# Another number of identity passes behind column sums, LRU gates and SSD products in a two-block sequence model

## The chip, the cores and the metric

The kernel runs on one core of one Trainium2 chip. The metric is the device time of one launch in microseconds, and the time of a kernel is the median of its runs. Engines are called TensorE (PE; its weight loads are PEld), VectorE (DVE), ScalarE (ACT), GpSimd (POOL) and SyncE (SP).

## What is computed

One sequence of 256 tokens with 2048 features goes through two blocks in float32. The first block has two layers: an RG-LRU beside an mLSTM, and an SSD layer. The second block has three branches (S5, gated linear attention, differential attention) and a feed-forward part. In short:

```python
def first_block(x, ...):
    x = x + lru_mlstm_layer(rmsnorm(x, e_norm[0]), ...)
    x = x + ssd_layer(rmsnorm(x, o_norm[0]), ...)
    return rmsnorm(x, final_norm)

def rglru(x, w_a, b_a, w_x, b_x, lam):            # 16 blocks of 128 features
    r = sigmoid(einsum('bsni,nij->bsnj', xb, w_a) + b_a)
    i = sigmoid(einsum('bsni,nij->bsnj', xb, w_x) + b_x)
    log_a = -8 * r * softplus(-lam)
    u = sqrt(-expm1(2 * log_a)) * (i * x)         # then a scan over the sequence

def ssd_scan(xh, dt, a, bm, cm):                  # 8 groups of 8 heads, chunks of 128 tokens
    y_diag = einsum('bcgls,bcgels,bcsgep->bclgep', cb, decay, xdt)
    ...

def rmsnorm(x, w):
    return x * rsqrt(mean(x * x, axis=-1) + 1e-6) * w
```

Nearly all the arithmetic is in the dense projections (`x @ w_in`, `y @ w_out`, the feed-forward matrices): 8048 blocks of 128 by 128 weights.

## The kernel before

Features lie on the partitions, tokens along the free dimension: an activation tile is 128 features by 256 tokens, and `[P, 2, T]` holds two of them. Each block of 128 by 128 weights is one step of `prod` (L285 to L293). Weights come by DMA in chunks of eight blocks (L250), ScalarE rounds four blocks at a time to the short float format (`wh`, L260), VectorE keeps the remainder (`wl`, L261). Activations are split alike, into `xh` and `xl`. A step is three matmuls of 128 x 256 into one PSUM tile `pm`: high by high (L291), high by low (L292), low by high (L293). The word *product* below means one such matmul; there are 3 x 8048 of them, in a fixed order that `_plan` lists.

The smaller work of a layer is written as generators that are put on a list; after each finished output tile `pump` advances each of them by one step, so their matmuls stand between those of the products. Within that, a scheduler sets the final order on each engine: it moves an instruction forward or back by its own estimate of when operands are ready. Its order is fixed when the program is built.

The words for what interrupts the products on TensorE:

- A *column sum* (`colsum`, L370 to L383) adds up squares over the partitions with matmuls of one column against a column of ones (L380). Each such matmul is two instructions in the trace. With `add` VectorE first adds the tiles into one (four instructions in all); without it there are two tiles (eight instructions).
- An *identity pass* (`align`, L389 to L393) transposes the identity into a PSUM tile `ps` that nobody reads. `colsum` ends with some of them, and so does each gate of the RG-LRU (L709).
- A *row pass* (`bcast`, L395 to L401): two transposes (L400) spread the 256 values that came out of a column sum, after a chain of small VectorE work (`rsqrt`), over all partitions.
- A *gate* of the RG-LRU (L697 to L709): matmuls by the two gate matrices (L704, L705).
- The *SSD products* (L1019 to L1028): for each of the eight groups, twice in the loop over `i`, sixteen matmuls that go in pairs to two halves of the array (L1027).

How many identity passes there are is set by three lines: a counter `aligned` runs through the calls, and

```python
        self.align(self.nalign() if add else 4)      # L382, in colsum
        return (1, 2, 4)[self.aligned % 3]           # L387, in nalign
        self.align(self.nalign())                    # L709, in rglru
```

so that successive places get 2, 4, 1, 2, 4, 1 and so on. A column sum without `add` (at the start of a layer, of a block and of the feed-forward part) always gets 4.

Of the kernel before, what the change touches and what calls it, by code (L numbers as in the profile page):

```python
# [150 lines left out]
class Builder:  # L151
    def __init__(self, nc, tc, d, dbg, ctx):
        self.nc, self.tc, self.d, self.dbg = nc, tc, d, dbg
        self.ctx = ctx
        self.uid = 0
        pool = lambda **k: ctx.enter_context(tc.tile_pool(**k))
        self.cst = pool(name="cst", bufs=1)

        self.gap(pool, 320)
        self.wp = pool(name="wp", bufs=1)  # L160
        self.gap(pool, 448)
        self.xp = pool(name="xp", bufs=1)
        self.tp = pool(name="tmp", bufs=1)
        self.gap(pool, 384)
        self.pm = pool(name="pm", bufs=1, space=PSUM)
        self.ps = pool(name="ps", bufs=1, space=PSUM)
        self.dr = pool(name="dr", bufs=1, space=DRAM)
        self.side = []
        self.aligned = 0

        self.plan = []
        at = {}
        for name, n in _plan():
            assert n % CH == 0, name
            for _ in range(n // CH):
                self.plan.append((name, at.get(name, 0)))
                at[name] = at.get(name, 0) + 1
        self.w_dma = 0
        self.w_split = 0
        self.w_pos = 0  # L180
        self.raw, self.hl = {}, {}
# [188 lines left out]
    def colsum(self, tiles, add=True):  # L370

        nc = self.nc
        while add and len(tiles) > 1:
            for i in range(len(tiles) // 2):
                nc.vector.tensor_tensor(tiles[i], tiles[i], tiles[len(tiles) - 1 - i], op=ALU.add)
            tiles = tiles[:len(tiles) // 2]
        p = self.pss((P, 2))
        for h in range(2):
            for i, t in enumerate(tiles):
                nc.tensor.matmul(p[:, h:h + 1], t[:, h * P:(h + 1) * P], self.con("ones", 0, 1),  # L380
                                 start=i == 0, stop=i == len(tiles) - 1)
        self.align(self.nalign() if add else 4)  # L382
        return p  # L383

    def nalign(self):
        self.aligned += 1
        return (1, 2, 4)[self.aligned % 3]  # L387

    def align(self, n):  # L389

# [299 lines left out]
    def rglru(self, i, u, lruw, sp, hb, yl):  # L690

        nc = self.nc
        x = self.tmp()
        for n in range(2):
            j = 2 * i + n
            self.conv(u[:, n], [self.par("conv_l_w", 16 * k + j) for k in range(4)],
                      self.par("conv_l_b", j), 4, x[:, n])  # L697
        yield

        a, g = self.tmp(), self.tmp()  # L700
        for n in range(2):
            j = 2 * i + n
            pr = self.pss()
            nc.tensor.matmul(pr[:, 0], lruw[:, n, 0:P], x[:, n], start=True, stop=True)  # L704
            nc.tensor.matmul(pr[:, 1], lruw[:, n, P:2 * P], x[:, n], start=True, stop=True)  # L705
            nc.scalar.activation(a[:, n], pr[:, 0], AF.Tanh, bias=hb[:, j:j + 1], scale=0.5)
            nc.scalar.activation(g[:, n], pr[:, 1], AF.Tanh, bias=hb[:, 16 + j:17 + j], scale=0.5)
        nc.vector.scalar_tensor_tensor(g, g, 1.0, x, op0=ALU.add, op1=ALU.mult)
        self.align(self.nalign())  # L709
        yield  # L710

        if self.lru is None:
            self.lru = self.st.tile([P, 4, T], F32, name=self.nm("lt"), tag="lt", bufs=1), []
        tt, todo = self.lru
        t = tt[:, 2 * len(todo):2 * len(todo) + 2]
        for n in range(2):
            nc.vector.tensor_scalar(a[:, n], a[:, n], 1.0, sp[:, 2 * i + n:2 * i + n + 1], op0=ALU.add, op1=ALU.mult)
        nc.scalar.activation(t, a, AF.Tanh, scale=-0.5)
        nc.scalar.activation(a, a, AF.Exp)
        nc.vector.scalar_tensor_tensor(g, a, 1.0, g, op0=ALU.add, op1=ALU.mult)  # L720
        todo.append((a, g, t))
        if i in LRU_ROOTS:
            self.lru = None
            yield
            tt = tt[:, 0:2 * len(todo)]
            nc.scalar.activation(tt, tt, AF.Sqrt, scale=0.25)
            for a, g, t in todo:
                nc.vector.tensor_tensor(g, g, t, op=ALU.mult)
                y = self.act()
                for n in range(2):  # L730
                    nc.vector.tensor_tensor_scan(y[:, n], a[:, n], g[:, n], 0.0, op0=ALU.mult, op1=ALU.add)
                yl.append(y)
        yield
# [245 lines left out]
    def ssd(self, g, bc, xs, tk, scr, yd):  # L979
        nc = self.nc  # L980
        csb = self.st.tile([P, 8, T], F32, name=self.nm("csb"), tag="csb", bufs=2)
        nc.gpsimd.dma_start(csb, scr[8 * g:8 * g + 8, :].unsqueeze(0).broadcast_to([P, 8, T]))

        S = self.pss((P, 384))
        nc.tensor.matmul(S[:, 0:256], bc[:, 0, 0:P], bc[:, 1, :], start=True, stop=True)
        nc.tensor.matmul(S[:, 256:384], bc[:, 0, P:T], bc[:, 1, P:T], start=True, stop=True)
        cb = self.act((P, 384))
        nc.vector.tensor_tensor(cb, S, self.con("tri3"), op=ALU.mult)

        xdt = []  # L990
        for hf in range(2):
            p = self.pss((P, 512))
            for i in range(2):
                for n in range(2):
                    c = 2 * i + n
                    nc.tensor.transpose(p[:, c * P:(c + 1) * P], xs[i][:, n, hf * P:(hf + 1) * P], self.con("ident"))  # L996
            o = self.act((P, 512))
            for e in range(8):
                nc.scalar.mul(o[:, 64 * e:64 * e + 64], p[:, 64 * e:64 * e + 64], tk[:, 2 + hf, 8 * g + e:8 * g + e + 1])
            xdt.append(o)  # L1000
        yield
        for i in range(2):
            dcs = []
            for e2 in range(2):
                dc = self.st.tile([P, 2, 384], F32, name=self.nm("dc"), tag="dc", bufs=3)
                for e in range(2):
                    ee = 4 * i + 2 * e2 + e
                    hd = 8 * g + ee

                    nc.vector.tensor_scalar(dc[:, e, 0:P], csb[:, ee, 0:P], tk[:, 0, hd:hd + 1], 0.0,  # L1010
                                            op0=ALU.add, op1=ALU.min)
                    nc.vector.tensor_scalar(dc[:, e, T:], csb[:, ee, P:T], tk[:, 1, hd:hd + 1], 0.0,
                                            op0=ALU.add, op1=ALU.min)
                    nc.scalar.activation(dc[:, e, P:T], csb[:, ee, P:T], AF.Exp, bias=tk[:, 0, hd:hd + 1])
                dv = dc.rearrange("p e (b l) -> p e b l", l=P)[:, :, 0::2, :]
                nc.scalar.activation(dv, dv, AF.Exp)
                nc.vector.tensor_tensor(dc, dc, cb.unsqueeze(1).broadcast_to([P, 2, 384]), op=ALU.mult)
                dcs.append(dc)
            yield  # L1019
            py = self.pss()  # L1020
            for t in range(2):
                for s in range(2):
                    for e in range(2):
                        ee = 4 * i + 2 * t + e
                        o = py[64 * e:64 * e + 64, t, :] if s == 0 else py[64 * e:64 * e + 64, t, P:T]
                        r = dcs[t][:, e, 0:256] if s == 0 else dcs[t][:, e, 256:384]
                        nc.tensor.matmul(o, xdt[s][:, 64 * ee:64 * ee + 64], r, start=s == 0, stop=s == 1,  # L1027
                                         tile_position=(0, 64 * e))  # L1028
            for n in range(2):
                nc.vector.scalar_tensor_tensor(xs[i][:, n], xs[i][:, n], self.par("d_skip", 4 * g + 2 * i + n),  # L1030
                                               py[:, n], op0=ALU.mult, op1=ALU.add)
            yd.append(xs[i])
            yield


# [727 lines left out]
```

## Time and profile before

| | |
|---|---|
| median of 3 runs | 3035.64 us |
| the three runs | 3035.18, 3035.64, 3041.25 us |
| the profiled execution | 3039.45 us, its span 3037.7 us |
| granted TensorE clock over the span | 0.997 |
| busy: TensorE matmul / weight load | 99% / 98% of the span |
| busy: VectorE / ScalarE / GpSimd | 75% / 58% / 3% |
| L260 ScalarE rounding of weights | 2013 times, 622 ns each |
| L261 VectorE remainder | 2013 times, 696 ns each |

How to read it: the first lines are times, the rest comes from one profiled execution. A busy share of 99% doesn't say how fast the engine goes while it is busy: the rows of matmuls overlap, each lasting some 0.28 us while the next begins after less than half of that. How fast it goes is read by counting the instructions in a stretch of known length. The granted clock is a fraction of the full 2.4 GHz.

### The profile page before, as it was taken

Reading aid. Unit: us, or ns where it says so; the run is one execution under the profiler, and the core shown is the slowest. Engines: PE = TensorE matmul, PEld = TensorE weight load, DVE = VectorE, ACT = ScalarE, POOL = GpSimd, SP = SyncE. Lnnn points to the kernel's source line nnn. Section 1 sums busy time; section 2 is a strip of 40 time slices with the busy share of each in tenths; the row PEclk is TensorE's granted clock in tenths of the full one; section 3 lists DMA queues with packets and bytes.
Section 4 is the critical chain, followed back from the end, with each engine's and each line's share of the span. In section 5 each row is a group of like instructions: output and inputs, shape, how many; then the busy total and the mean of one; then the engine's idle time right before and its main releaser. Section 6 shows DMA issues by size and latency. Waiting matters only on the chain.

```text
span 3037.7 us, 67061 instructions
## 1 busy us (share of the span) xinstructions
PE 3012.5 (99%) x26390; PEld 2963.1 (98%) x26390; DVE 2291.7 (75%) x4693; ACT 1748.2 (58%) x3303; POOL 90.4 (3%) x123
## 2 busy tenths in 40 slices
PE   8999999999999999999999999999999999999998
PEld 8999999999999999999999999999999999999998
DVE  8787866779999777778888686676677776577764
ACT  6776545556677555565555554555555555455554
POOL 1000000010000000120000000000010000000000
PEclk9999999999999999999999999999999999999999
DMA  6665556666665556665555554556666666665564
GB/s 232 185 189 164 186 160 194 194 189 213 192 194 181 175 184 191 192 203 180 156 158 160 168 162 153 168 166 215 195 190 188 187 188 187 188 186 186 186 187 152
DMA packets 153933, 556.30 MB, mean 183 GB/s; under 512 B 17392, under 2 KB 18544, under 8 KB 152592
## 3 DMA queue, kind: packets, MB, share of 16 engines
q1 hardware_dynamic: 148752, 534.89, 56.8%
q0 software_dynamic: 3104, 14.75, 1.3%
q8 instruction: 206, 3.38, 0.4%
q10 hardware_dynamic: 1760, 2.38, 0.3%
q14 instruction: 111, 0.91, 0.1%
HBM read 547.69 MB, written 4.26 MB: 182 GB/s over the span
## 4 chain that ended last, share of the span: by engine, by line
PE 98%; DVE 1%; DMA 0%; issue 0%; ACT 0%; SPq 0%; DVEq 0%; ACTq 0%
PE pm L291 31%; PE pm L292 30%; PE pm L293 30%; PE ps L1027 1%; PE ps L1329 0%; PE ps L1367 0%; PE ps L1488 0%; PE ps L380 0%; DVE wl L261 0%; PE ps L393 0%; PE ps L1314 0%; PE ps L1259 0%; PE ps L821 0%; PE ps L996 0%; PE ps L704 0%
## 5 line engine op out<-in xcount | busy, mean ns | idle before, releaser
L260 ACT CAST wh<-w 128x512 fp32r<-128x512 f32 (+1 forms) x2013 | 1237.6, 622 | 1138.8 <-PE pm L292 849.5
L261 DVE TENSOR_TENSOR wl<-w,wh 128x512 fp32r<-128x512 f32 (+1 forms) x2013 | 1387.5, 696 | 587.7 <-ACT wh L260 571.1
L291 PE MATMUL pm<-x,wh 128*128 128x256 f32 x5504 | 1541.9, 280 | 6.0 <-ACT wh L260 5.7
L293 PE MATMUL pm<-x,wl 128*128 128x256 f32 x5504 | 1535.2, 279 | 3.3 <-DVE q L448 3.2
L292 PE MATMUL pm<-x,wh 128*128 128x256 f32 x5504 | 1536.4, 279 | 1.5 <-DVE x L509 1.5
L291 PEld LDWEIGHTS pm<-x,wh 128*128 128x128 f32 x5504 | 1035.4, 188 | 15.1 <-issue 7.9
L293 PEld LDWEIGHTS pm<-x,wl 128*128 128x128 f32 x5504 | 1042.9, 190 | 6.6 <-DVE q L448 3.4
L292 PEld LDWEIGHTS pm<-x,wh 128*128 128x128 f32 x5504 | 1036.1, 188 | 4.1 <-issue 1.9
L291 PE MATMUL pm<-a,wh 128*128 128x256 f32 x1712 | 479.0, 280 | 0.5 <-ACT wh L260 0.5
L292 PE MATMUL pm<-a,wh 128*128 128x256 f32 x1712 | 477.7, 279 | 0.3 <-DVE a L344 0.3
L293 PE MATMUL pm<-a,wl 128*128 128x256 f32 x1712 | 477.9, 279 | 0.0
L293 PEld LDWEIGHTS pm<-a,wl 128*128 128x128 f32 x1712 | 324.6, 190 | 0.1
L291 PEld LDWEIGHTS pm<-a,wh 128*128 128x128 f32 x1712 | 322.0, 188 | 0.9 <-ACT wh L260 0.7
L292 PEld LDWEIGHTS pm<-a,wh 128*128 128x128 f32 x1712 | 321.5, 188 | 0.6 <-DVE a L344 0.5
L291 PE MATMUL pm<-h,wh 128*128 128x256 f32 x576 | 162.4, 282 | 1.8 <-DVE t L1113 1.8
L292 PE MATMUL pm<-h,wh 128*128 128x256 f32 x576 | 161.3, 280 | 0.0
L293 PE MATMUL pm<-h,wl 128*128 128x256 f32 x576 | 161.0, 280 | 0.0
L291 PEld LDWEIGHTS pm<-h,wh 128*128 128x128 f32 x576 | 109.7, 190 | 5.8 <-issue 3.1
L292 PEld LDWEIGHTS pm<-h,wh 128*128 128x128 f32 x576 | 109.0, 189 | 0.9 <-issue 0.8
L293 PEld LDWEIGHTS pm<-h,wl 128*128 128x128 f32 x576 | 108.6, 189 | 0.0
L439 DVE SCALAR_TENSOR_TENSOR a<-t,ocw,a 128x255 f32<-128x255 f32 (+1 forms) x144 | 64.5, 477 | 17.8 <-ACT a L437 17.8
L293 PE MATMUL pm<-b,wl 128*128 128x256 f32 x256 | 70.7, 276 | 0.0
(432 smaller groups left out, 2431.1 us busy)
## 6 DMA issues: line engine op xcount, KB each, us to landing
w<-w_up SPq DMA_DIRECT2D x172, 512.0 KB, 3.5
w<-w_w_in_u SPq DMA_DIRECT2D x114, 512.0 KB, 3.7
w<-w_o_in SPq DMA_DIRECT2D x98, 512.0 KB, 4.0
w<-w_w_in_g SPq DMA_DIRECT2D x96, 512.0 KB, 3.5
w<-w_down SPq DMA_DIRECT2D x86, 512.0 KB, 3.6
w<-w_e_in_z SPq DMA_DIRECT2D x64, 512.0 KB, 3.5
w<-w_e_out SPq DMA_DIRECT2D x64, 512.0 KB, 3.5
w<-w_o_z SPq DMA_DIRECT2D x64, 512.0 KB, 3.5
```

Of the source, the lines that this page charges most:

```text
L260: nc.scalar.copy(h[:, s], w[:, s])
L261: nc.vector.tensor_tensor(l[:, s], w[:, s], h[:, s].bitcast(F32), op=ALU.subtract)
L291: nc.tensor.matmul(o, h, xh(k), start=k == 0, stop=False)
L292: nc.tensor.matmul(o, h, xl(k), start=False, stop=False)
L293: nc.tensor.matmul(o, l, xh(k), start=False, stop=k == KT - 1)
L439: nc.vector.scalar_tensor_tensor(dst[:, j:], u[:, :T - j], ws[taps - 1 - j], dst[:, j:], op0=ALU.mult, op1=ALU.add)
L1027: nc.tensor.matmul(o, xdt[s][:, 64 * ee:64 * ee + 64], r, start=s == 0, stop=s == 1, tile_position=(0, 64 * e))
```

## The change

Three places are edited. The counter and `nalign` go. Every column sum is followed by one pass, every gate of the RG-LRU by two. In each SSD group the first of the two sets of products (`i == 0`) is now followed by one pass, the second by none.

```diff
-        self.aligned = 0
...
-        self.align(self.nalign() if add else 4)
+        self.align(1)
         return p
-
-    def nalign(self):
-        self.aligned += 1
-        return (1, 2, 4)[self.aligned % 3]
...
         nc.vector.scalar_tensor_tensor(g, g, 1.0, x, op0=ALU.add, op1=ALU.mult)
-        self.align(self.nalign())
+        self.align(2)
         yield
...
             yd.append(xs[i])
+            if i == 0:
+                self.align(1)
             yield
```

Since lines go, L291 to L293 are L290 to L292 in the changed kernel, L380 is L379, L393 is L388, L400 is L395 and L1027 is L1022. The orders of DMA issues on SyncE and GpSimd are the same in both programs; the scheduler moves some products, and some work of ScalarE and VectorE, past the interruptions.

On TensorE, behind the column sum at the start of the feed-forward part (`r` and `t` are the two tiles of squares, `pm` the product tile), before:

```order
L292 MATMUL pm_31822<-b_30746,wh_31875 128x256
L293 MATMUL pm_31822<-b_30745,wl_31876 128x256
L380 MATMUL ps_31975<-consts,r_30977 128x1
L393 MATMUL ps_31980<-consts 128x128 x4
L291 MATMUL pm_32012<-x_30969,wh_31893 128x256
L292 MATMUL pm_32012<-x_30970,wh_31893 128x256
```

and after:

```order
L291 MATMUL pm_31802<-b_30726,wh_31855 128x256
L292 MATMUL pm_31802<-b_30725,wl_31856 128x256
L379 MATMUL ps_31955<-consts,r_30957 128x1
L388 MATMUL ps_31960<-consts 128x128
L290 MATMUL pm_31989<-x_30949,wh_31873 128x256
L291 MATMUL pm_31989<-x_30950,wh_31873 128x256
```

Four passes have become one; the rest of the sum comes 44 products later instead of 41.

On TensorE, the rest of that sum (three matmuls in the program, six instructions in the trace), before:

```order
L291 MATMUL pm_32012<-x_31812,wh_31943 128x256
L292 MATMUL pm_32012<-x_31813,wh_31943 128x256
L380 MATMUL ps_31975<-consts,t_31969 128x1
L380 MATMUL ps_31975<-consts,r_30977 128x1
L380 MATMUL ps_31975<-consts,t_31969 128x1
L293 MATMUL pm_32012<-x_31812,wl_31944 128x256
```

and after:

```order
L290 MATMUL pm_31989<-x_31943,wh_31923 128x256
L291 MATMUL pm_31989<-x_31944,wh_31923 128x256
L379 MATMUL ps_31955<-consts,t_31949 128x1
L379 MATMUL ps_31955<-consts,r_30957 128x1
L379 MATMUL ps_31955<-consts,t_31949 128x1
L292 MATMUL pm_31989<-x_31943,wl_31924 128x256
```

This piece is the same. The row passes follow 49 products behind it instead of 46, and then come 6099 products instead of 6105.

On TensorE, the first SSD products of the second group (`dc` the decayed scores, `a` the inputs by tokens), after; before, the row of L388 is not there:

```order
L1022 MATMUL ps_10415<-dc_10246,a_10223 64x256 x2
L1022 MATMUL ps_10415<-dc_10246,a_10237 64x128 x2
L1022 MATMUL ps_10415<-dc_10255,a_10223 64x256 x2
L1022 MATMUL ps_10415<-dc_10255,a_10237 64x128 x2
L388 MATMUL ps_10426<-consts 128x128
L290 MATMUL pm_10460<-x_7933,wh_10349 128x256
```

One pass has come in between the last SSD product and the next product.

## Rows read from the trace of the kernel before

**Rows 1.** The page: span, busy time by engine, chain that ended last.

```profile
span 3037.7 us, 67061 instructions
...
PE 3012.5 (99%) x26390; PEld 2963.1 (98%) x26390; DVE 2291.7 (75%) x4693; ACT 1748.2 (58%) x3303; POOL 90.4 (3%) x123
...
PE 98%; DVE 1%; DMA 0%; issue 0%; ACT 0%; SPq 0%; DVEq 0%; ACTq 0%
```

**Rows 2.** Windows, TensorE: from:to us, length, busy (xinstructions), granted clock, DMA share, GB/s.

```profile
28.40:73.90 45.50, 45.50 (x389) 1.00 0.67 221
...
460.65:660.45 199.80, 199.80 (x1765) 1.00 0.63 193
...
1113.50:1189.75 76.25, 76.25 (x675) 1.00 0.62 193
...
2078.00:2293.00 215.00, 215.00 (x1899) 1.00 0.65 203
...
2304.54:3023.65 719.11, 719.11 (x6108) 1.00 0.59 184
```

**Rows 3.** Lines by form, TensorE: count | busy us, mean ns of one | idle.

```profile
L393 PE MATMUL ps<-consts 128*128 128x128 f32 x80 | 14.4, 282 | 0.0
```

**Rows 4.** Timeline, TensorE: start us, length us; behind two, four and one passes.

```profile
1007.14 0.41 PE L393 MATMUL ps<-consts 128*128 128x128 f32 x2
1007.31 0.36 PE L291 MATMUL pm<-x,wh 128*128 128x256 f32 x1
...
1031.54 0.63 PE L393 MATMUL ps<-consts 128*128 128x128 f32 x4
1031.92 0.36 PE L293 MATMUL pm<-x,wl 128*128 128x256 f32 x1
...
1055.21 0.31 PE L393 MATMUL ps<-consts 128*128 128x128 f32 x1
1055.27 0.37 PE L293 MATMUL pm<-x,wl 128*128 128x256 f32 x1
```

**Rows 5.** Waits of TensorE from 3020 us on: us in total, times, longest.

```profile
PE ps L400 <- DVE s L367: 2.0, 1, 2.0
```

**Rows 6.** Windows, TensorE, in the norm stage of layer two and behind it.

```profile
1057.00:1065.00 8.00, 8.00 (x73) 1.00 0.55 192
...
1103.00:1113.00 10.00, 10.00 (x87) 1.00 0.53 162
...
1215.00:1224.00 9.00, 9.00 (x79) 1.00 0.58 175
...
1260.00:1335.00 75.00, 75.00 (x640) 1.00 0.68 210
```

**Rows 7.** Windows, TensorE, at the feed-forward's start: before and behind six column-sum matmuls.

```profile
2299.20:2304.30 5.10, 5.10 (x46) 1.00 0.56 199
2293.90:2298.20 4.30, 4.30 (x40) 1.00 0.63 220
```

**Rows 8.** Timeline, TensorE: the last of the six matmuls, and the row passes.

```profile
2298.68 0.36 PE L380 MATMUL ps<-consts,t 128*128 128x1 f32 x2
2298.91 0.36 PE L293 MATMUL pm<-x,wl 128*128 128x256 f32 x1
...
2304.41 0.38 PE L400 MATMUL ps<-consts,s 128*128 128x128 f32 x2
```

**Rows 9.** Windows, TensorE, at the start of layer two.

```profile
661.20:665.70 4.50, 4.50 (x41) 1.00 0.62 200
...
673.00:691.00 18.00, 18.00 (x162) 1.00 0.66 203
```

**Rows 10.** Windows, TensorE, behind a gate with two passes.

```profile
182.70:188.50 5.80, 5.80 (x52) 1.00 0.43 136
```

**Rows 11.** Windows, TensorE, behind the first and the second SSD products of a group.

```profile
804.00:814.00 10.00, 10.00 (x91) 1.00 0.86 281
817.00:827.00 10.00, 10.00 (x87) 1.00 0.57 175
```

## The prediction

> **What bounds the kernel now.** I read the page first. TensorE is busy for 99% of the span and holds 98% of the chain that ended last, almost all of it on the three product lines L291 to L293 [rows 1]. So the time is the number of TensorE instructions times their pitch (the time from the start of one to the start of the next), and whatever shortens the pitch of the products is worth its full size.
>
> Next I read the windows of long stretches that hold nothing but products. A matmul row lasts 0.28 us, so a window also counts the ones that straddle its edges: the pitch is (length + 0.28) / count. The stretch from 460.65 has (199.80 + 0.28) / 1765 = 113.4 ns, the ones from 1113.50 and 2078.00 also 113.4 ns. The stretch from 2304.54 to 3023.65, the whole feed-forward part, has 719.39 / 6108 = 117.8 ns, and the window from 28.40 has 45.78 / 389 = 117.7 ns [rows 2]. Same instruction, same shape, granted clock 1.00 in all of them, no idle time: the products run at one of **two pitches**, 4.4 ns (3.9%) apart, and keep one for hundreds of microseconds. I call them fast and slow. What changes between two stretches is only the short work of another form that interrupts them: column sums (L380), identity passes (L393), row passes (L400), gates, SSD products. So I take it that an interruption hands the stretch behind it one of the two pitches, and that the number of identity passes is part of what decides.
>
> **Part 1: the passes themselves.** The trace has 80 identity passes [rows 3]; the built change has 46 (22 behind column sums, 16 behind the gates, 8 new ones behind SSD products). From the first pass to the next product it is 0.06 us with one pass, 0.17 with two, 0.38 with four [rows 4], so a pass costs (0.38 - 0.06) / 3 = 0.107 us. Of the 34 that go, 3 stand in the last column sum, where TensorE waits 2.0 us for VectorE anyway [rows 5]; they give nothing. 31 x 0.107 = **-3.3 us**.
>
> **Part 2: column sums in the norm stage of layer two (1007 to 1247 us).** Here the number of passes rotates through 2, 4, 1. Behind one pass the products are fast: 8.28 / 73 = 113.4 ns from 1057. Behind four they are slow at 1103, 10.28 / 87 = 118.2 ns, and behind two at 1215, 9.28 / 79 = 117.5 ns [rows 6]. Over the whole trace, one pass behind a column sum of one tile is followed by fast products in six places of six, two passes by slow ones in five of five, four by either. A pair of row passes (L400) keeps a fast stretch fast: both longest fast stretches begin directly behind such a pair [rows 2]. So with one pass everywhere, the eight slow stretches of this stage (96, 104, 88, 104, 88, 98, 94 and 88 products, 760 in all) should turn fast: 760 x 4.4 ns = **-3.3 us**. Three slow stretches behind other column sums (58, 57 and 48 products) give another 163 x 4.4 = **-0.7 us**.
>
> **Part 3: where layers change (2293 us, and the like at 660 us).** The scheduler lets the identity passes run behind the first matmuls of the sum, then 41 products, then the other six matmuls of the sum (L380), 46 products, the two row passes, and the long stretch. After the change it is one pass, 44 products, the six, 49 products, the row passes, 6099 products. At 2293.9 the products are fast, 4.58 / 40 = 114.5 ns with a few slower ones at the start; behind the six they are slow, 5.38 / 46 = 117.0 ns [rows 7]. The six and the row passes follow with nothing between them and the products [rows 8], and neither moves. If one pass also leaves the 44 products fast, the six matmuls meet the same fast stretch as before and should again hand on the slow pitch. The slow pitch has a pattern of three products, so a slow stretch longer by three (49 for 46) reaches the row passes as before. So I take **0** for the feed-forward part. By the same reasoning the 660 us place gets worse: there the first stretch is slow now, 4.78 / 41 = 116.6 ns, and behind the six it is fast, 18.28 / 162 = 112.8 ns further on [rows 9]. With a fast first stretch the six hand on slow: 50 + 171 products slower, 40 faster, 181 x 4.4 = **+0.8 us**.
>
> **Part 4: the gates (74 to 290 us).** Passes of 2, 4, 1 in turn become 2 everywhere. From a fast stretch two passes give slow products at 182.7, 6.08 / 52 = 116.9 ns [rows 10]; that stretch is only 51 long. Three stretches of 472, 472 and 160 products stand behind a gate that is split by five products, with two passes in place of 1, 4 and 2, and all three are fast now; for one with two passes the trace shows fast, for the other two nothing. Bounds: -1.7 us (the 384 products before the first gate turn fast, since the first column sum now has one pass) and +4.9 us (1104 products turn slow). I take **+1.0 us**, nearer to no change because the one example with two passes is fast.
>
> **Part 5: the SSD products (724 to 997 us).** Each of eight groups has two interruptions by L1027. Behind the first the 96 products are fast, 10.28 / 91 = 113.0 ns at 804; behind the second slow, 10.28 / 87 = 118.2 ns at 817 [rows 11]. The new pass goes behind the first. No row shows a pass there. Bounds: +3.4 us (8 x 96 products turn slow) and -3.4 us (the second interruption, met in another state, hands on fast). I take 0, the first staying fast. The new passes write a PSUM buffer that nobody reads; the nearest case, the passes behind column sums, shows no gap [rows 4], and what VectorE does behind L1027 waits for the products, not for the pass.
>
> **Part 6: what may flip by itself.** The 768 products from 1247 are slow (75.28 / 640 = 117.6 ns from 1260 [rows 6]) although they begin fast. Whether that recurs no row tells: 0 or -3.4 us, I take 0. The stretch of 398 from 1356, behind a double column sum, may turn slow: 0 or +1.8 us, I take 0.
>
> **Sum:** -3.3 - 3.3 - 0.7 + 0.8 + 1.0 = -5.5 us. The profiled execution took 3039.45 us (span 3037.7 and 1.75 outside it), 3.8 above the median of 3035.64, so it is itself one of the longer runs; the same difference on the median gives **3030.1 us**. On the unknown terms alone it lies between 3022 and 3038.
>
> **Rivals.**
> *The feed-forward part turns fast.* It decides at the six matmuls behind the 44 products: if the first stretch is left slow, or the six hand on fast, 6099 x 4.4 = 26.8 us go as well: 3003.3. For it: at 660 us the six did hand on fast, from a slow stretch. Against it: from a fast stretch, the case expected here, the only example hands on slow. Chance 0.21.
> *Slower.* The pair of row passes behind a one-pass sum hands on slow where today it hands on fast, at 460, 1113 and 2078 us: 1765 + 675 + 1899 products, 4339 x 4.4 = 19.1 us, less the 5.5: 3049.2. It decides from two of the three long ones on. Against it: two of the three have one pass today, and their surroundings hardly move. Chance 0.05.
> *The passes don't set the pitch.* The two pitches may belong to the stage (operands, what else runs) and not to what interrupts. Then only Part 1 counts: 3035.64 - 3.3 = 3032.3. Against it: within the norm stage the same products change pitch from stretch to stretch [rows 6]. Chance 0.08. The Trainium skill, "TensorE: Matmul & The Clock Gate", section "Back-to-back issue gap", goes further: at the full clock a matmul follows the one before after its columns over 2.4 GHz plus 2.5 ns, one fixed value, an estimate of 109 ns for 256 columns. By it no pass could change the pitch. The trace does not agree: 113.4 and 117.8 ns, both at a granted clock of 1.00.
>
> **How the numbers follow.** 0.2% of the median, 6.1 us, is about what a measurement of this kernel can tell from no change. The forecast has 0.66, and its 3030.1 lies just inside that bound; with its unknown terms I give 0.27 of it to faster (below 3029.6), 0.37 to same, 0.02 to slower. The feed-forward rival adds 0.21 to faster, the slower one 0.05 to slower, the third 0.08 to same: 0.48, 0.45, 0.07. The forecast's own range is 3022 to 3038. That alone would leave out more than 2 in 10, so the range reaches down to the feed-forward rival with a few microseconds for the same unknowns: 3000 to 3039.
>
> **What would show it.** In the changed trace: 46 identity passes; a pitch of 113.4 ns in every stretch from 1007 to 1247; behind the six L380 matmuls at the feed-forward's start 117.8 ns as now; about 220 slower products behind the six at 660 us. The prediction is wrong if the long stretch from about 2300 us shows 113.4 ns, if one of the stretches from 460 or 2078 us shows 117.8 ns, or if stretches behind one pass are not alike.

## The result, and the profile after

The changed kernel takes 3007.39 us (median; 3001.16 to 3009.96), the kernel before 3035.44 us beside it (3035.18 to 3041.25). The ratio is 0.990, with a 95% interval of 0.988 to 0.9921: 28 us less. The kernel before was measured anew beside each round of experiments (medians of 3041.97, 3041.21 and 3038.27 us), so runs of different rounds are compared by their ratios. The time lies in the range, but the forecast was 3030.1 us. The case that came true is the first rival, the feed-forward part turning fast (3003.3 us), with the gates turning out worse than I took them.

The page of the changed kernel, in the parts of [rows 1]: hardly anything but the span has moved, and TensorE is still 99% busy. The last row is from the lines by form (count | busy us, mean ns of one | idle), and answers [rows 3]: 46 passes, as built.

```profile
span 3003.4 us, 66986 instructions
...
PE 2979.5 (99%) x26356; PEld 2930.9 (98%) x26356; DVE 2293.3 (76%) x4693; ACT 1747.5 (58%) x3303; POOL 90.5 (3%) x123
...
L388 PE MATMUL ps<-consts 128*128 128x128 f32 x46 | 12.6, 302 | 0.0
```

From here on most rows are windows of TensorE: from:to us, length, busy (xinstructions), granted clock, DMA share, GB/s. I read windows of one length against each other, since their counts then say the pitch directly. A window of 4.40 us holds 39 or 40 products at the slow pitch (4.68 / 117.8 ns) and 41 or 42 at the fast one (4.68 / 113.4 ns); 10 us hold 87 or 91; 690 us hold 5861 or 6090.

First the feed-forward part of the changed kernel: the 44 products behind the first matmuls of the column sum, the 49 behind the other six, and the long stretch behind the row passes.

```profile
2286.45:2290.85 4.40, 4.40 (x39) 1.00 0.70 222
2292.25:2296.65 4.40, 4.40 (x41) 1.00 0.56 200
2298.00:2988.00 690.00, 690.00 (x6090) 1.00 0.62 191
```

Slow, fast, fast, where [rows 7] and [rows 2] had fast, slow, slow. The granted clock is 1.00 in all of them, before and after. The long stretch began at 2304.54 and ended at 3023.65 us before; it now runs from 2297.7 to 2989.1 us. That is 27.8 us less, 0.7 of it because six products now lie ahead of the row passes.

Other windows of the changed kernel. The first two are the long stretches that [rows 2] shows fast; the next three answer [rows 6]; then the three stretches at the start of layer two [rows 9], and the two SSD groups [rows 11].

```profile
466.00:665.70 199.70, 199.70 (x1764) 1.00 0.63 193
2080.00:2280.00 200.00, 200.00 (x1767) 1.00 0.66 196
...
1105.00:1115.00 10.00, 10.00 (x91) 1.00 0.62 187
1216.00:1225.00 9.00, 9.00 (x81) 1.00 0.58 181
1260.00:1335.00 75.00, 75.00 (x664) 1.00 0.72 218
...
666.30:670.70 4.40, 4.40 (x40) 1.00 0.61 219
672.00:676.40 4.40, 4.40 (x41) 1.00 0.56 188
680.00:690.00 10.00, 10.00 (x91) 1.00 0.58 177
...
809.00:819.00 10.00, 10.00 (x91) 1.00 0.88 283
822.00:832.00 10.00, 10.00 (x87) 1.00 0.58 178
```

The norm stage is fast throughout, and so are the 768 products behind it (664 in 75 us against 640). The 660 us place is as it was: slow, fast, fast. So are the SSD groups: fast, slow.

The stretches behind the gates, four windows of 15 us, which hold about 130 slow or 135 fast products:

```profile
85.00:100.00 15.00, 15.00 (x130) 1.00 0.65 205
135.00:150.00 15.00, 15.00 (x130) 1.00 0.65 211
200.00:215.00 15.00, 15.00 (x129) 1.00 0.67 210
262.00:277.00 15.00, 15.00 (x129) 1.00 0.59 184
```

All four are slow. In the trace of before the same four stretches are fast (134 or 135 in 15 us). For the first of the four that isn't the change's doing: four runs below are the kernel before up to 2293 us, with the same order on TensorE, and in three of their profiled executions this stretch is slow too. This is the one with one pass behind the feed-forward's row passes:

```profile
85.00:100.00 15.00, 15.00 (x130) 1.00 0.64 211
```

The other three stretches are fast in all four.

**Where the 34.3 us between the two profiled executions went** (3037.7 and 3003.4 us), from the starts of the stretches in both traces: the gates and the stage behind them, 76 to 466 us, +5.1; 466 to 1012 us, 0.0; the norm stage, -3.4; the 672 products and what follows to 1248 us, -0.8; the 768 and what follows to 1354 us, -3.7; from there to 2298 us, -4.2; the long feed-forward stretch, -27.8; the start and the end together, +0.5. Of the -4.2, 2.5 stand in one stretch around 1810 us, and they are not the change's: in the run before, TensorE stood still longer there (1.80 us without work against 0.85), and the granted clock fell behind the stop. The row of before comes first, that of after second:

```profile
1755.00:1821.00 66.00, 64.20 (x537) 0.97 0.55 172
...
1752.00:1815.00 63.00, 62.15 (x535) 1.00 0.58 176
```

The medians lie 28 us apart and not 34, because the profiled execution of before (3039.45 us) lies 4.0 us above its median and that of after (3005.22 us) 2.2 below.

### The profile page after: what moved, and what is told of

Same layout as the page of the kernel before. It is cut to its first block, busy times and chain, and to the rows that moved or that the text cites. A ratio compares the mean times of both kernels' runs of the same rounds, so it can differ in the third digit from the quotient of the medians.

```text
span 3003.4 us, 66986 instructions
## 1 busy us (share of the span) xinstructions
PE 2979.5 (99%) x26356; PEld 2930.9 (98%) x26356; DVE 2293.3 (76%) x4693; ACT 1747.5 (58%) x3303; POOL 90.5 (3%) x123
## 4 chain that ended last, share of the span: by engine, by line
PE 98%; DVE 1%; DMA 0%; issue 0%; ACT 0%; SPq 0%; DVEq 0%
PE pm L290 31%; PE pm L291 30%; PE pm L292 30%; PE ps L1022 1%; PE ps L1326 0%; PE ps L1364 0%; PE ps L1485 0%; PE ps L379 0%; DVE wl L260 0%; PE ps L1311 0%; PE ps L1256 0%; PE ps L388 0%; PE ps L816 0%; PE ps L991 0%; PE ps L699 0%; PE ps L700 0%
## 5 line engine op out<-in xcount | busy, mean ns | idle before, releaser
L290 PE MATMUL pm<-x,wh 128*128 128x256 f32 x5504 | 1537.7, 280 | 5.6 <-ACT wh L259 5.5
L292 PE MATMUL pm<-x,wl 128*128 128x256 f32 x5504 | 1532.1, 279 | 3.5 <-DVE wl L260 3.4
L291 PE MATMUL pm<-x,wh 128*128 128x256 f32 x5504 | 1531.8, 278 | 1.0 <-DVE x L504 1.0
L290 PEld LDWEIGHTS pm<-x,wh 128*128 128x128 f32 x5504 | 1039.6, 189 | 13.2 <-ACT wh L259 6.3
L292 PEld LDWEIGHTS pm<-x,wl 128*128 128x128 f32 x5504 | 1038.3, 189 | 6.3 <-DVE wl L260 4.1
L291 PEld LDWEIGHTS pm<-x,wh 128*128 128x128 f32 x5504 | 1037.6, 189 | 3.3 <-issue 1.9
L290 PE MATMUL pm<-a,wh 128*128 128x256 f32 x1712 | 476.2, 278 | 0.5 <-ACT wh L259 0.5
L292 PE MATMUL pm<-a,wl 128*128 128x256 f32 x1712 | 475.1, 278 | 0.0
L291 PE MATMUL pm<-a,wh 128*128 128x256 f32 x1712 | 474.3, 277 | 0.4 <-DVE a L343 0.4
L290 PEld LDWEIGHTS pm<-a,wh 128*128 128x128 f32 x1712 | 322.2, 188 | 0.8 <-ACT wh L259 0.7
L291 PEld LDWEIGHTS pm<-a,wh 128*128 128x128 f32 x1712 | 321.7, 188 | 0.7 <-DVE a L343 0.6
L292 PEld LDWEIGHTS pm<-a,wl 128*128 128x128 f32 x1712 | 322.0, 188 | 0.0
L290 PE MATMUL pm<-h,wh 128*128 128x256 f32 x576 | 161.1, 280 | 0.8 <-DVE t L1110 0.8
L291 PE MATMUL pm<-h,wh 128*128 128x256 f32 x576 | 159.9, 278 | 0.0
L292 PE MATMUL pm<-h,wl 128*128 128x256 f32 x576 | 159.7, 278 | 0.0
L290 PEld LDWEIGHTS pm<-h,wh 128*128 128x128 f32 x576 | 108.5, 188 | 4.8 <-issue 3.1
L291 PEld LDWEIGHTS pm<-h,wh 128*128 128x128 f32 x576 | 108.2, 188 | 0.9 <-issue 0.8
L292 PEld LDWEIGHTS pm<-h,wl 128*128 128x128 f32 x576 | 108.2, 188 | 0.0
L291 PE MATMUL pm<-b,wh 128*128 128x256 f32 x256 | 70.8, 276 | 0.0
```

The costliest lines, as they stand in the source:

```text
L290: nc.tensor.matmul(o, h, xh(k), start=k == 0, stop=False)
L291: nc.tensor.matmul(o, h, xl(k), start=False, stop=False)
L292: nc.tensor.matmul(o, l, xh(k), start=False, stop=k == KT - 1)
```

## The experiments

The theory at this point: an interruption hands the next stretch its pitch by the moment at which it ends. The rivals: fewer passes are better; a pass as such does it; the long stretch is fast for another reason (its operands, its place in the program).

**The feed-forward sum with four passes again.** The changed kernel, but the one column sum ahead of the feed-forward part keeps four passes.

```diff
-    def colsum(self, tiles, add=True):
+    def colsum(self, tiles, add=True, n=1):
...
-        self.align(1)
+        self.align(n)
...
-        rstd = self.row(self.rsqrt(self.mean_eps(self.colsum(self.acc, False), D), 2))
+        rstd = self.row(self.rsqrt(self.mean_eps(self.colsum(self.acc, False, 4), D), 2))
```

> The changed kernel with four passes instead of one behind the column sum at the feed-forward's start, nothing else. Theory (the interruption just ahead hands the stretch its pitch): the 44 products in between become 41 fast ones, the six L380 matmuls hand on the slow pitch as in the kernel before, and the 6105 products behind the row passes go at 117.8 ns: 3007.4 + 27 = about 3034 us. Rival (what the edits farther up leave behind made the feed-forward part fast): the stretch stays at 113.4 ns, about 3007.7 us. Rival (only the passes' own work counts): 3 x 0.107 more, 3007.7 us.

Measured: 3032.21 us (3029.91 to 3034.35), 0.9968 of before (0.9956 to 0.998). The windows of first, second and long stretch:

```profile
2288.15:2292.55 4.40, 4.40 (x41) 1.00 0.50 172
2293.55:2297.95 4.40, 4.40 (x39) 1.00 0.54 192
2299.10:2989.10 690.00, 690.00 (x5861) 1.00 0.58 187
```

Fast, slow, slow, as before the change. Three passes of 0.107 us, put in 12 us ahead of it, decide on the pitch of 6100 products. All other edits of the change, together with the stretches that fall either way (Part 6 below), make up the remaining 0.3%.

**The kernel before with one pass there.** The mirror image: only this sum of the kernel before gets one pass.

```diff
-    def colsum(self, tiles, add=True):
+    def colsum(self, tiles, add=True, n=4):
...
-        self.align(self.nalign() if add else 4)
+        self.align(self.nalign() if add else n)
...
-        rstd = self.row(self.rsqrt(self.mean_eps(self.colsum(self.acc, False), D), 2))
+        rstd = self.row(self.rsqrt(self.mean_eps(self.colsum(self.acc, False, 1), D), 2))
```

> The kernel before with one pass instead of four behind the column sum at the feed-forward's start, nothing else. Theory: the 44 products in between are slow, the six L380 matmuls hand on the fast pitch, 6099 products at 113.4 ns: 3035.4 - 27.1 = about 3008 us. Rival (edits farther up are needed too): no change beyond 0.3 us, about 3035 us.

Measured: 3012.36 us (3008.72 to 3013.76), ratio 0.9902 (0.9887 to 0.9917). The first and the long stretch:

```profile
2295.35:2299.75 4.40, 4.40 (x40) 1.00 0.59 209
...
2307.00:2997.00 690.00, 690.00 (x6091) 1.00 0.59 191
```

Nearly the whole gain of the change is in this one line.

**Passes added, nothing taken away.** If fewer passes were better, adding some must not help. The kernel before with two passes behind the feed-forward part's row passes:

```diff
         rstd = self.row(self.rsqrt(self.mean_eps(self.colsum(self.acc, False), D), 2))
+        self.align(2)
```

> The kernel before with two identity passes added directly behind the feed-forward's row passes, nothing removed: 0.2 us more work on the engine that is never idle. Theory (where an interruption ends within a fixed grid of about 6.7 ns decides): the interruption ends 262 cycles of 0.83 ns later, which moves its end on the grid by 6 of 8 places, to one from which the trace of before always shows fast products. The 6105 products go at 113.4 ns, 3035.4 + 0.2 - 27 = about 3009 us. Rival (fewer passes are faster): 3035.6 us. Rival (the column sum must be followed by one pass): 117.8 ns and 3035.6 us.

Measured: 3015.07 us (3013.89 to 3016.55), ratio 0.9913 (0.9898 to 0.9928); the long stretch:

```profile
2308.60:2998.60 690.00, 690.00 (x6090) 1.00 0.60 191
```

27 us less with more work. "Fewer is better" has fallen.

**One pass in the same place.** If any short work there helped, one pass must do too. To forecast this and the run on 124 columns I used the start times of the trace, which are in whole nanoseconds (the rows here print 10 ns). Within every fast stretch the products start at one place of a grid of 6.667 ns (the fast pitch, 113.33 ns, is 17 of its steps); I count the place of a start in eight steps of 0.833 ns. A pass takes 109 ns from start to start, 131 steps, so it moves what follows by three places (131 = 16 x 8 + 3). In the trace of before, the first product behind these row passes starts at place 6 and the stretch is slow.

```diff
         rstd = self.row(self.rsqrt(self.mean_eps(self.colsum(self.acc, False), D), 2))
+        self.align(1)
```

> The kernel before with one identity pass, instead of two, behind the row passes of the feed-forward part; nothing else. Theory (a pass shifts where the next product starts, and only some of the shifts give the fast pitch; in the trace of before the first product behind these row passes starts at a place from which two passes reach a fast one and one pass a slow one): the 6105 products stay slow at 117.8 ns, and the time stays at that of before plus 0.1 us, about 3042 us on this chip. Rival (any short work put between the row passes and the products makes them fast): 113.4 ns, about 27 us less, 3015 us.

Measured: 3040.86 us against 3041.21 of before, ratio 1.0003 (0.9991 to 1.0014). Slow:

```profile
2306.60:2996.60 690.00, 690.00 (x5861) 1.00 0.59 187
```

**The same pass, four columns shorter.** This sets the end of the interruption apart from the number of passes. The edit is shown against the run with one pass; it takes four rows off the pass along with four columns.

```diff
-    def align(self, n):
+    def align(self, n, w=P):
...
-            self.nc.tensor.transpose(p, self.con("ident"), self.con("ident"))
+            self.nc.tensor.transpose(p[:, 0:w], self.con("ident")[0:w], self.con("ident")[0:w, 0:w])
...
-        self.align(1)
+        self.align(1, 124)
```

> As the run with one identity pass behind the feed-forward part's row passes (kernel before otherwise), but this pass goes over 124 columns instead of 128. Theory (what counts is where the interruption ends; 4 columns less move that end by 4 cycles of 0.83 ns, which turns the slow place of the 128-column pass into a fast one): the 6105 products at 113.4 ns, about 27 us less than before, some 3014 us. Rivals (the number of passes decides, or a pass is a pass): slow as with 128 columns, some 3041 us.

Measured: 3013.35 us (two runs, 3011.36 and 3015.34), ratio 0.9919 (0.9898 to 0.994). The first row is the pass in the lines by form, the second the window of the long stretch:

```profile
L393 PE MATMUL ps<-consts 124*128 124x124 f32 x1 | 0.3, 273 | 0.0
...
2303.90:2993.90 690.00, 690.00 (x6090) 1.00 0.62 191
```

A pass of 124 columns is followed by fast products where one of 128 is followed by slow products, and the kernel is 25 us faster than the kernel before beside it. No count of passes explains that. In the start times the first product begins 141 ns after the second row pass, against 138 ns with 128 columns: 3 ns later, although the pass should end 3 ns earlier by its columns. On a grid of 6.667 ns the two are the same place, and the trace can't tell which it was; nor does a run set the shape of the pass apart from the moment of its end. The place of the first product behind the interruption, worked out from the start times (a place is good to about 0.7):

```
row passes, then                 expected from 6     read    stretch of 6105
nothing (before)                 -                   5.9     slow
one pass of 128 columns          6 + 3 -> 1          1.3     slow
two passes                       6 + 6 -> 4          3.6     fast
one pass of 124 columns          6 + 7 -> 5          5.0     fast
```

**Two passes at the feed-forward sum.** Does only "one" work there? The edit is that of the first experiment with 2 for 4.

> The changed kernel with two passes instead of one behind the column sum that begins the feed-forward part. Theory (two passes move the start of the next product from one slow place to another slow one; the six matmuls of the sum met from a slow stretch hand on a fast one, as in the changed kernel and at 660 us): first stretch slow, second and the 6100 products fast, time that of the changed kernel. Rival (only one pass gives the fast long stretch, or the fewer the passes the better): 6100 x 4.4 = 27 us more, some 3034 us.

Measured: 3002.57 us (two runs, 3002.36 and 3002.78), ratio 0.9878 (0.985 to 0.9907). First, second and long stretch:

```profile
2284.15:2288.55 4.40, 4.40 (x40) 1.00 0.62 214
2289.95:2294.35 4.40, 4.40 (x42) 1.00 0.59 198
2295.80:2985.80 690.00, 690.00 (x6090) 1.00 0.60 191
```

Slow, fast, fast, like one pass. So at this sum one and two passes do well and four do badly; in every run of this study the long stretch is fast if the first one is slow, and slow if the first one is fast, as long as nothing is put behind the row passes.

**The rotation put back in the one-tile sums.** Meant to measure Part 2 by itself: the changed kernel with 2, 4, 1 behind column sums of one tile, one pass behind the others.

```diff
+        self.aligned = 0
...
-        self.align(1)
+        self.align(self.nalign() if add else 1)
...
+    def nalign(self):
+        self.aligned += 1
+        return (1, 2, 4)[self.aligned % 3]
```

> The changed kernel with the rotation (2, 4, 1 passes) put back behind the column sums of one tile alone; the layer sums, the gates and the SSD products stay as changed. Theory: in the norm stage (about 1010 to 1250 us) the stretches behind two and behind some of the four passes turn slow again, some 760 products, and perhaps the 768 behind it: 3 to 7 us more than the changed kernel, and the feed-forward part stays fast, so about 3010 to 3014 us. Rival (the pitch of this stage has another cause than the passes): all its stretches stay at 113.4 ns.

Measured: 3046.63 us, ratio 1.002 (1.0009 to 1.0031): slower than the kernel before, 33 us more than I expected at the most. A stretch of the norm stage, the stretch from 2078 us, and the long feed-forward stretch:

```profile
1013.00:1023.00 10.00, 10.00 (x87) 1.00 0.47 157
...
2090.00:2290.00 200.00, 200.00 (x1700) 1.00 0.59 187
...
2315.20:3005.20 690.00, 690.00 (x5861) 1.00 0.58 187
```

The norm stage did what I expected. What I missed is that the last one-tile sum of the program, ahead of the stretch from 2078 us, also gets two passes by the rotation, and that the pitch is handed on from there.

**That one sum alone.** The changed kernel with one pass more at this place; every TensorE instruction keeps its place in the order.

```diff
+        self.sums = 0
...
-        self.align(1)
+        self.sums += 1
+        self.align(2 if self.sums == 20 else 1)
```

> The changed kernel with two passes instead of one behind a single column sum, the one ahead of the 1887 products at 2072 us; no other instruction moves. Theory: the 66 products behind it and the 1887 behind their row passes turn slow (1953 x 4.4 = 8.6 us), as in the run with the rotation put back. What the feed-forward part then does hangs on its first stretch of 44: if that is slow, as in the changed kernel, the 6099 stay fast and the time is about 3015 us; if it is fast, as in the run with the rotation put back, they turn slow and the time is about 3042 us. Rival (these long stretches do not hang on this pass): no change, 3006 us.

Measured: 3041.19 us (3036.69 to 3043.45), 1.0005 of before (0.9995 to 1.0016). The 66 products behind the sum, the 1887 behind their row passes, then the three stretches of the feed-forward part:

```profile
2067.50:2074.50 7.00, 7.00 (x62) 1.00 0.71 207
2080.00:2280.00 200.00, 200.00 (x1700) 1.00 0.62 190
...
2297.95:2302.35 4.40, 4.40 (x41) 1.00 0.61 213
2303.65:2308.05 4.40, 4.40 (x40) 1.00 0.56 209
2309.60:2999.60 690.00, 690.00 (x5861) 1.00 0.60 187
```

Slow (7 us hold 64 of them in the changed kernel), slow, fast, slow, slow. One pass of 0.107 us costs the whole gain of the change: by the pitches 8.6 us in the stretches directly behind it and 27 in the feed-forward part, whose own passes have not been touched, and some 32 us by the ratios (1.0005 against 0.990). So the gain also hangs on the pitch with which the 1887 products arrive.

**The gates with four and one passes.** The changed kernel, four passes behind a whole gate and one behind a gate that is split by five products (23 passes in all behind the eight gates, for 16).

```diff
-        self.align(2)
+        self.align(1 if i in (2, 4, 6) else 4)
```

> The changed kernel with four passes behind the gates that are not split and one behind the three that are split by five products, instead of two everywhere: one pass more in all (17 for 16... 20 and 3 against 10 and 6). Theory: the stretches of 360, 474, 474 and 162 products behind the gates, slow in the changed kernel's trace, all go at 113.4 ns: 1470 x 4.4 = 6.5 us less, about 3001 us against 3007.4. Rival (the slow gates come from the stretch before the first gate being fast, whatever the passes): they stay slow, 3008 us.

Measured: 2999.09 us (2997.04 to 2999.95), ratio 0.9859 (0.9842 to 0.9875), the best of all. The four windows of 15 us in the stretches behind the gates:

```profile
85.00:100.00 15.00, 15.00 (x135) 1.00 0.62 203
135.00:150.00 15.00, 15.00 (x135) 1.00 0.64 203
200.00:215.00 15.00, 15.00 (x135) 1.00 0.53 186
255.00:270.00 15.00, 15.00 (x135) 1.00 0.58 191
```

All four are fast, with seven passes more. The 1464 products at stake are worth 6.5 us, less 0.7 for the passes; the ratios differ by 0.0041, some 12 us, their intervals lying just clear of each other. The trace shows the size of the gates' own part: from the 360 products to the 1762 it is 390.0 us in the changed kernel and 384.0 here. The rest of the 12 us I cannot name; the run with two passes at the feed-forward sum has the gates of the changed kernel and a ratio of 0.9878, so about half of the 12 us lies between runs with the same gates. In this trace the 312 products ahead of the first gate are slow, so for the first gate alone the rival is not excluded here; the last experiment, with the same gates, excludes it.

**Without the SSD passes.** The changed kernel without the eight new ones.

> The changed kernel without the eight new passes behind the SSD products. Theory: behind the first product group of a pair the 96 products are fast with the pass and, as in the kernel before, fast without it; the second stays slow; the only gain or loss is the passes' own 8 x 0.107 = 0.9 us, unless the part behind 1000 us is handed another pitch. Time within 2 us of the changed kernel. Rival (the new pass is what keeps the first group fast): 8 x 96 x 4.4 = 3.4 us more.

Measured: 3006.79 us (two runs), ratio 0.9892 (0.9863 to 0.9921), not to be told apart from the changed kernel's 0.990. Here is one of the pairs in the middle, the first group and the second:

```profile
849.00:859.00 10.00, 10.00 (x91) 1.00 0.85 273
862.00:872.00 10.00, 10.00 (x87) 1.00 0.55 173
```

Fast, slow, with the pass and without it. In the first two pairs the two change roles (slow, fast), which is worth nothing; in the third both are slow, and so are two stretches of about 40 products at 757 and 796 us, some 0.8 us in all. The new passes bring nothing that a run shows.

**A pass behind the second SSD group too**, with the gates of four and one.

```diff
-            if i == 0:
-                self.align(1)
+            self.align(1)
```

> The changed kernel with four passes and one behind the gates in place of two (as in the run on the gates), and with a pass behind the second SSD group of each pair too. Theory: the second groups, met from a fast stretch like the first, turn fast: 8 x 96 x 4.4 = 3.4 us less the passes' own 0.9 us, so about 2996 to 2998 us. Rival (the pass does not carry over to the second group): 3000 us or a little more.

Measured: 2999.96 us (2996.87 to 3002.28), ratio 0.9871 (0.9855 to 0.9888): no gain over the run on the gates alone (2999.09 us). Again a first and a second group, and then the stretch behind the first gate:

```profile
803.00:813.00 10.00, 10.00 (x91) 1.00 0.82 272
816.00:826.00 10.00, 10.00 (x91) 1.00 0.56 160
...
85.00:100.00 15.00, 15.00 (x135) 1.00 0.66 208
```

Both groups are fast now, as expected, in the seven pairs that have 96 products behind the second group (3.0 us); behind the eighth, 118 products are slow. But eight passes cost 0.9 us by the length taken above, three stretches of about 40 products ahead of the second, third and fourth pair turn slow (750, 789 and 827 us), the last pairs are cut up differently by the scheduler, and a stretch of 162 at 1490 us is slow, as it is in the trace of before. Part of what one interruption gains is lost behind the next. The stretch behind the first gate is fast here, with the 312 products ahead of it fast too: four passes do that, and not the pitch on arrival.

## Why the prediction was right and wrong

The range held, but by the rival that it had been stretched to include: the sum of the forecast missed by 22.7 us, and its account of the feed-forward part was wrong.

**The two pitches, and that passes decide** (the basis): right at the places that were tried. The rival that the passes don't set the pitch has fallen with the runs that change one sum. But passes are not all that decides: see Part 6. The fixed distance that the Trainium skill states ("TensorE: Matmul & The Clock Gate", "Back-to-back issue gap"; an estimate of 109 ns here) does not hold for these products: 690 us at a granted clock of 1.00 held 5861 in one run and 6090 in another of the same instruction. The same section of the Trainium skill gives that distance for a matmul by itself, and says that in a stream of weight loads and matmuls both set the spacing; this kernel is such a stream, so the prediction read more into it than it says.

**Part 1**: 46 passes, as said. No run separates their own time from what they do to the pitch. A first pass behind a column sum lasts 0.31 us and a further one 0.27 in both traces; the mean rose from 282 to 302 ns because fewer further ones are left and the new ones behind SSD products last 0.33.

**Part 2**: right for the norm stage. All stretches from 1012 to 1248 us are fast. The stretch from the first of these sums to the 672 products takes 103.2 us for 106.7; I had 3.0 for the slow products of its seven slow stretches and 0.9 for its eight passes less. Of the three stretches elsewhere, those at 395 and 1998 us turned fast and the one at 419 us, behind one pass like the others but met from a slow stretch, did not:

```profile
419.50:426.50 7.00, 7.00 (x61) 1.00 0.50 154
```

(A fast stretch has 64 here.) So stretches behind one pass are not alike, which I had named as a sign that the prediction is wrong; the feed-forward part is the costly case of it.

**Part 3, the feed-forward part: wrong, and this is more than the whole miss** (26.8 us by the pitches, of which the gates took some back). The step that failed is "if one pass also leaves the 44 products fast". The evidence for it was six sums of six with one pass, but they were sums of one tile, whose matmuls all run ahead of the passes. Here only the first two matmuls of the sum run ahead, so the interruption is shorter, and one pass ends it elsewhere:

```profile
2285.88 0.28 PE L379 MATMUL ps<-consts,r 128*128 128x1 f32 x2
2286.01 0.31 PE L388 MATMUL ps<-consts 128*128 128x128 f32 x1
2286.07 0.36 PE L290 MATMUL pm<-x,wh 128*128 128x256 f32 x1
```

(Timeline of the changed kernel: start us, length us. The first sum matmul begins 0.20 us ahead of the next product; with one pass behind a sum of one tile, as at 1012 us, it is 0.42 us.) That the end of the shorter interruption is the cause is argued from this; what the runs show is the slow stretch. The first stretch came out slow, and the six then handed on fast, which is what the trace of before showed for a slow first stretch at 660 us [rows 9] and what I had named as the rival's condition. The step behind it was right: given a fast first stretch, the six hand on slow, as the run with four passes shows. A warning stood in the rows, and I weighed it too low: [rows 7] and [rows 9] show this form of sum twice, with four passes both times and a fast stretch ahead both times, and the products behind the passes are fast at 2293 us and slow at 661. No row showed the form with one pass. The step deserved an even chance, and the feed-forward rival with it more than 0.21.

**Part 3, the 660 us place**: by the same error +0.8 expected, 0 measured; the three windows are as before.

**Part 4, the gates**: mis-sized. I took +1.0 us between -1.7 and +4.9; it is +5.1 from 76 to 466 us, just outside. All four stretches turned slow, 1464 products. Two things were off. The 360 behind the first gate (1.6 us) were in neither bound, since this gate keeps its two passes; but the 312 ahead of it now arrive fast instead of slow. They do so too in the three runs of the kernel before up to 2293 us in which the 360 are slow, so this part isn't the change's; without it the gates come to +3.5, inside the bounds. And the one example with two passes behind a split gate, on which I leaned, was met from a slow stretch (52 products) and is now met from a fast one. In both, the same passes met another pitch on arrival.

**Part 5, the SSD products**: right, 0.

**Part 6**: the 768 products turned fast (-3.4; I had 0). They do this or not by themselves: slow in the run with one pass more at 2066 us, where nothing ahead of them differs from the changed kernel, fast in the run with 124 columns, where nothing ahead of them differs from the kernel before. So a single trace can't credit this stretch to the change. The first row is from the run with one pass more, the second from the run with 124 columns:

```profile
1260.00:1335.00 75.00, 75.00 (x639) 1.00 0.68 211
1260.00:1335.00 75.00, 75.00 (x664) 1.00 0.68 216
```

The start times show where it falls: the first 36 products are fast in all these traces; within the next ten, where two products of another input (`a`) stand between those of `h`, three starts in a row lie about 0.2 us behind the one before, and what follows is slow or fast. The same holds at 1093 us, where TensorE stops twice for an input (0.8 us without work in all): in the trace of before the products are slow ahead of and behind these stops, in the run with one pass behind the row passes they are slow ahead of them and fast behind. The 672 from 1113 us, fast in the trace of before, are slow in the four other runs that are the kernel before up to there. So a short halt of the products can hand on either pitch as well, with no pass involved. The 398 at 1356 us stayed fast, as taken.

**The slower rival** (the row passes hand on slow at 460, 1113 or 2078 us) did not come true, but the run with one pass more shows that row passes can hand on the slow pitch at 2078 us when they are met from a slow stretch, and that one pass is enough for it: it gave 3041 us.

**What stays open.** The four runs of the changed kernel lie 9 us apart. Part of it is stretches that fall either way, such as the 768, and the clock at the start; I have not traced it run by run. Why one form of sum with four passes gave slow products at 661 us and fast products at 2293, both from fast, is not settled either: the first products start at places 2.9 and 3.5 by the start times, which lie too close together to be told apart surely. Nor do I know why the grid has the step it has; I can only say that the places forecast the three runs behind the row passes. They don't settle every stretch: by the same reckoning the long feed-forward stretch of the changed kernel starts at place 2.9 and is fast, and the 1887 products of the run with one pass more start at 3.2 and are slow.

## What to carry to other kernels

Where a kernel is one long row of equal matmuls, compute the pitch of every long stretch from its count and length before looking for idle time: a busy share of 99% hid 27 us here. When two pitches show, look at what interrupts just ahead of the stretch, a short stop for an input included, and try one or two short dummy passes there. Such a gain is brittle, since any later edit ahead of it can undo it; check the long stretches again after every edit, and carry evidence only between interruptions of the same form and from the same pitch on arrival.

## What the hardware showed that I had not expected

- A difference of some 3 ns in an interruption goes with the pitch of thousands of matmuls behind it: 128 against 124 columns in one pass, 3040.86 us (ratio 1.0003) against 3013.35 (0.9919). The pitch then lasts for 691 us without a pause.
- More work can be faster: two passes added, 27 us less.
- The pitch is handed on across interruptions. One pass at 2066 us changed the feed-forward part at 2309 us, with 2046 products and four interruptions between.
- The granted clock stood at 0.50 (1.2 of 2.4 GHz) in the changed kernel's profiled run until 32 us, after the engine had waited for its first inputs. Rows of 2 us hold 11 products there, where the kernel before holds 19 at a granted clock of 1.00, some 1.8 us in all:

```profile
28.00:30.00 2.00, 2.00 (x11) 0.50 1.02 404
30.00:32.00 2.00, 2.00 (x11) 0.50 1.06 419
```
